# Eight gate products moved from the gate steps into four projections, and branch B's results read before the merge

## The chip, the core and the metric

The kernel runs on one core of one Trainium2 chip. The metric is the device time of one execution in microseconds (us), from the device's own clock. The kernel before took 1479.22 us (median of three runs, 1477.01 to 1479.26).

## What is computed

One layer of an encoder with 1024 tokens of width 1024, and 16 meta tokens ahead of them (1040 rows). All inputs are float32. The part that matters here is the mixer:

```python
proj = h @ w_in                     # qa, ka, va, qb, kb, vb, ga, gb
y_a = differential_attention(qa, ka, va, ...)   # 4 heads, all keys
y_b = windowed_gqa(qb, kb, vb, sink)            # 8 heads, 2 key heads, window 128
merged = jax.nn.sigmoid(ga) * (y_a @ w_ba) + jax.nn.sigmoid(gb) * (y_b @ w_bb)
h = h + merged @ w_o
h = h + (jax.nn.silu(n @ w_gate) * (n @ w_up)) @ w_down     # n = rms_norm(h)
out = rms_norm(h)
```

Here h is normalised ahead of the first product. The gates ga and gb are the columns of w_in from 2304 and from 3328 on, 1024 each.

## The kernel before

**Operands.** Every product runs in fp32r with split operands: a float32 tile is split into a rounded high part (on ACT, ScalarE) and the remainder as low part (on POOL, GpSimd, or on DVE, VectorE), in `split` (L118 to L120). A product is then three matmuls: high by high, high by low, low by high. The normalised, transposed input lies in SBUF as hT_hi and hT_lo.

**Projections.** `prep` (L176) reads 128 columns of w_in into a tile w and splits them into wh and wl; there are two of each. `ensure` prepares the next entry of the list `order`, one projection ahead of the one that runs; entries in `on_vector` are split on DVE, the others on POOL. `project_a(h)` projects q, v and k of head h of branch A. The results leave PSUM by ACT and DVE into tiles of `stage` (tag qk, three rooms, named qk_stage, va_stage and gate_first) and go to DRAM by DMA (qa_d, va_d, ka_d). All DMAs are issued by SP, in an order fixed when the program is built; each DMA takes one of eight completion semaphores in turn and waits for the DMA eight before it.

**Gate products.** ga and gb are not computed in a plain way but with seven products instead of eight for each 2 x 2 block of blocks. The two gates are cut into 8 groups k of 256 columns; for each there are products p = 1 to 7, each of 128 columns by 512 tokens over 512 rows. Some take sums of weight blocks (ws_d, prepared on POOL during branch B, `weight_sums`) and sums of token blocks (ts_d, `token_sums`, read over a quarter of hT by `load_sums` when that quarter is no longer needed). Product p = 2 takes no sums: weights of rows 512 to 1023, first 128 columns of the group, and tokens as they are (`quad(., 1, 0)`). One product is four steps of three matmuls with 512 columns; `gate_steps` (L716) is a generator of such steps, `g_load` reads the weights of a product (tile gr, five rooms), `g_split` splits them into gop (four rooms), and the result goes to g_d in DRAM, by an ACT copy, or by an addition on DVE to what g_d held (gk).

**What runs when.** Branch B's attention overlaps the projections of heads 2 and 3 of branch A (POOL's order is the written one there, other engines are ordered by a scheduler when the program is built). Then come the products of p = 2 with k = 0 to 3 (w_g, w_gop, L699 and L744: `G_EARLY`), then those with k = 4 to 7 (gr, gop, `G_FIRST` = 16 steps) ahead of head 0's first score, then attention of branch A: 32 tiles of 128 queries, in which PE's order is written by hand. `SLOTS` says in which order a tile's score chunks (s), gate steps (g), transposes (t) of the tile before, and value products or the tail (n) follow each other; `SLOTS_MORE` has one gate step more and is used for the first four tiles. Heads 1 to 3 begin with `G_HEAD` = 10 gate steps. `HOLD` = 30 steps are kept for the tail, after the last tile (L911). In the iteration after tile 31 (only transposes) no step is left.

**Merge.** After the gate steps y_b @ w_bb and y_a @ w_ba are computed (`branch_mm`, L769, PSUM tile ppa), each multiplied with its sigmoid. Branch B's results have been in DRAM (yb_d) since before attention. They are read into four rows of the tile tb (L958) and split into yb (L964), and the first two weight blocks of w_bb are read into another part of tb (L954). tb lies in room that attention used. The other weight blocks and y_a are read into a ring that lies where hT was, so these DMAs wait for the last gate matmul.

Of the kernel before, what the change touches and what calls it, by code (L numbers as in the profile page):

```python
# [19 lines left out]
P = 128  # L20
# [20 lines left out]
SLOTS_MORE = "sgsgsngsgsgstntnt"  # L41
# [6 lines left out]
HOLD = 30  # L48
N_MORE = 4
# [3 lines left out]
G_FIRST = 16  # L53
G_EARLY = 4
# [21 lines left out]
def encoder_block(ctx: ExitStack, tc: tile.TileContext, x, meta, norm_mix, w_in, lq1, lk1, lq2, lk2,  # L76
# [117 lines left out]
    on_vector = order[on_vector:] + [C_QB]  # L194
    prepped = {}

    def ensure(n):
        while order and len(prepped) < n:
            col = order.pop(0)
            prepped[col] = prep(col, f"c{col}", lo_eng=nc.vector if col in on_vector else None)  # L200
# [59 lines left out]

    vtpool, close_vt = pool("vtpool")
    lowpool, close_low = pool("lowpool")
    bpool, close_bpool = pool("bpool")
    kb = [(bpool if g else lowpool).tile([P, 2, NT, 144], F32R, tag=("k1", "kb")[g], name=f"kb{g}", bufs=1) for g in range(BG)]
    vb = [(bpool if g else lowpool).tile([P, 9, P], F32R, tag=("q1", "vb")[g], name=f"vb{g}", bufs=1) for g in range(BG)]
# [313 lines left out]
    G_ACT = {2: (1, 0), 5: (0, 1), 3: (1, 1), 1: (0, 0), 6: (1, 0), 7: (0, 1), 4: (1, 1)}  # L579
    G_OUT = {2: (0, 0), 5: (1, 1), 3: (0, 1), 1: (0, 0), 6: (0, 1), 7: (1, 1), 4: (1, 0)}  # L580
    order_g = [(2, k) for k in range(8)]
# [35 lines left out]
    def g_load(n, raw=None):  # L617
        p, k = order_g[n]
        if raw is None:
# [3 lines left out]
                          g_weights(k, *{2: (1, 0), 1: (0, 0), 4: (1, P)}[p], P))  # L623
# [33 lines left out]
    def load_a1(h):  # L657
        q = [None, lowpool.tile([P, S], F32R, tag="q1", name=f"aq{h}_1", bufs=1)]
# [52 lines left out]
    flush_v()  # L711
    order_pool.__exit__(None, None, None)

    gpools = []

    def gate_steps():  # L716
        for n, (p, k) in enumerate(order_g):
            if gpools:
                g_ahead(n + 1)
            op, act = g_ready.pop((p, k)), G_ACT[p]  # L720
            if p in (2, 5, 1):
                g_bank[k] = pp_bank(f"pg{p}_{k}")
            ps = g_bank[k]
            for c in range(4):
                for i, (a, b) in enumerate(((0, 0), (0, 1), (1, 0))):
                    nc.tensor.matmul(ps, op[:, a, c], quad(b, *act)[:, c], start=(p in (2, 5, 1) and c == 0 and i == 0),  # L726
                                     stop=(p in (2, 3, 4) and c == 3 and i == 2), skip_group_check=True)
                if c == 3:
# [3 lines left out]
                    else:  # L732
                        if gpools:
                            st = gpool.tile([P, 512], F32, tag="g", name="gate_stage", bufs=G_BUFS)
                        else:
                            st = f32(stage.tile([P, 2, 512], F32R, tag="qk", name="gate_first", bufs=QK_BUFS))[:, 0]
# [8 lines left out]
    for _ in range(4 * G_EARLY):  # L745
        next(gates)
# [5 lines left out]
    gpools.append(gpool)  # L752
# [3 lines left out]
    apool2, close_apool2 = pool("apool2")  # L756


    def branch_w(p, o, src, nme, raw=None):
        w = (raw_tile(f"wbr{nme}_{o}")[:, 0:512] if raw is None else raw).rearrange("p (c n) -> p c n", n=P)  # L760
        nc.sync.dma_start(w, src[:, o * P:(o + 1) * P].rearrange("(c p) n -> p c n", p=P))
# [87 lines left out]

    n_gates = [4 * (len(order_g) - G_EARLY) - HOLD]  # L850

# [28 lines left out]
    for n in range(AH * NT + T_LAG):  # L880
        scoring, turning = iter(()), iter(())
        if n < AH * NT:
# [5 lines left out]
            if t % 2 == 0:  # L888
                at_ = apool2.tile([P, 9, 2, 256], F32R, tag="at", name=f"at{h}_{t}", bufs=AT_BUFS)
# [5 lines left out]
        for what in SLOTS_MORE if n < N_MORE else SLOTS:  # L895
# [8 lines left out]
        for _ in scoring:  # L904
            pass
        for _ in turning:
# [3 lines left out]
    n_gates[0] += HOLD  # L910
    while tail:  # L911
        step_tail()
        fill(3)
    order_pe.__exit__(None, None, None)
    close_apool2()
    close_apool()
    close_low()
    close_vt()
    fill(1000)
    ypool, close_ypool = pool("ypool")  # L920
    close_psum2()
# [28 lines left out]
    tb = ypool.tile([P, DC, S], F32, name="tb")  # L950
    ya0pool, close_ya0 = pool("ya0pool")
    ybpool, close_yb = pool("ybpool")

    first_w = [branch_w(ypool, o, w_bb, "b", tb[:, 2, o * 512:o * 512 + 512]) for o in range(2)]  # L954

    yb_t = []
    for j in range(4):
        nc.sync.dma_start(tb[:, 4 + j, :], yb_d[j])  # L958
        yb_t.append(ybpool.tile([P, 2, S], F32R, name=f"yb{j}"))
        if j % 2:  # L960
            for h in range(2):
                cols = slice(h * 512, h * 512 + 512)
                for k in (j - 1, j):
                    split(yb_t[k][:, 0, cols], yb_t[k][:, 1, cols], tb[:, 4 + k, cols], nc.vector)  # L964
# [31 lines left out]
    for o in range(DC):  # L996
        w = first_w[o] if o < 2 else branch_w(ypool, o, w_bb, "b")
        for half in range(2):
            gt, ps, tk = gated(0, o, half, w, yb)
            nc.vector.tensor_tensor(tb[:, o, tk], gt, ps, ALU.mult)  # L1000
# [15 lines left out]
    for n, (o, half) in enumerate(order_a):  # L1016
# [4 lines left out]
        nc.gpsimd.tensor_tensor(gt, gt, tb[:, o, tk], ALU.add)  # L1021
# [5 lines left out]
    close_ypool()  # L1027

# [461 lines left out]
```

## Time and profile before

| | |
|---|---|
| median of three runs | 1479.22 us |
| the profiled execution | 1477.96 us |
| its span, first to last instruction | 1476.2 us |
| PE busy | 1435.2 us, 97% |
| DVE, ACT, POOL busy | 60%, 46%, 44% |
| mean granted clock of TensorE | 0.988 |
| PE waits, by far the largest group (first gate products) | 8.4 + 6.7 us |

The stages by PE's timeline: branch B with the projections to 306, the products of p = 2 to 353, attention to 621, its tail with the last gate steps to 645, the merge from 649. How to read the views: a wait is listed as "engine, tile, line <- what it waited for: us in total, times, longest us". A line of a timeline has start, duration, engine, line, operation, output <- inputs, shape and count; in brackets stands the idle time before it and what ended it. A line of windows has the window, its length, the busy time and number of instructions of PE, PE's weight loads, DVE, ACT and POOL, then the granted clock, the share of the DMA engines and GB/s. L119 and L120 are the two lines of `split`, for whatever tile. Rows of a busy PE overlap, since matmuls are pipelined; the distance of starts is the pace.

### The profile page before, as it was taken

How to read it: one execution, taken by the hardware profiler on the slowest of the kernel's cores; microseconds unless marked ns; L12 is line 12 of the kernel's file. 1: busy time of each engine (PE TensorE's matmuls, PEld its weight loads, DVE VectorE, ACT ScalarE, POOL GpSimd, SP SyncE). 2: the span in 40 equal slices, each digit the busy share in tenths (PEclk: the TensorE clock that was granted, in tenths of full speed). 3: DMA queues.
4: the chain of work that ended last, by engine and by line, in shares of the span. 5: the costliest groups of instructions: out<-in, count | busy, mean ns of one | idle time of the engine just before them, and what ended most of it. 6: DMA issues, size and time to landing. Idle time of an engine off the chain costs nothing.

```text
span 1476.2 us, 21253 instructions
## 1 busy us (share of the span) xinstructions
PE 1435.2 (97%) x7279; PEld 1226.9 (83%) x7279; DVE 888.0 (60%) x1618; ACT 682.0 (46%) x1293; POOL 650.7 (44%) x614
## 2 busy tenths in 40 slices
PE   8999999978999999999999999999999999999997
PEld 7998989966998899868788878888888888888886
DVE  7478436513879788743522876655555554777667
ACT  6366435524666555544511653333333333444454
POOL 5599127734333433333822475554544452000444
PEclk9999999989999999999999999999999999999999
DMA  8368768776276655277541433333322233964433
GB/s 240 87 204 240 211 167 252 236 245 232 94 247 205 225 176 173 74 251 219 182 149 58 142 110 127 128 107 101 107 100 98 96 107 107 325 217 135 130 124 140
DMA packets 189692, 242.42 MB, mean 164 GB/s; under 512 B 19008, under 2 KB 116736, under 8 KB 189584
## 3 DMA queue, kind: packets, MB, share of 16 engines
q1 hardware_dynamic: 189584, 241.07, 50.7%
q8 instruction: 57, 0.93, 0.3%
q14 instruction: 51, 0.42, 0.1%
HBM read 157.45 MB, written 77.00 MB: 159 GB/s over the span
## 4 chain that ended last, share of the span: by engine, by line
PE 79%; POOL 6%; DVE 5%; issue 4%; DMA 4%; ACT 1%; SPq 1%; POOLq 0%; ACTq 0%; DVEq 0%
PE pg L1271 27%; PE pg L726 9%; PE pd L1365 8%; PE po L1048 6%; PE ppa L769 5%; PE aps L785 4%; PE apy L824 3%; PE pp_qb L211 3%; POOL oa L120 3%; PE pp_va L211 2%; PE pp_qa L211 2%; PE apt L811 2%; PE pp_ka L211 1%; PE bpt L351 1%; PE bps L326 1%
## 5 line engine op out<-in xcount | busy, mean ns | idle before, releaser
L120 POOL TENSOR_TENSOR wop<-wf,wop 128x512 fp32r<-128x512 f32 x128 | 173.3, 1358 | 165.2 <-ACT wop L119 150.7
L1271 PE MATMUL pg<-t,wop 128*128 128x512 f32 x1056 | 242.6, 389 | 0.0
L1271 PEld LDWEIGHTS pg<-t,wop 128*128 128x128 f32 x1056 | 198.2, 188 | 41.2
L1365 PE MATMUL pd<-ob,oa 128*128 128x512 f32 x924 | 210.2, 389 | 0.7 <-POOL oa L120 0.4
L1365 PEld LDWEIGHTS pd<-ob,oa 128*128 128x128 f32 x924 | 173.3, 188 | 37.5 <-POOL oa L120 0.9
L1271 PE MATMUL pg<-b,wop 128*128 128x512 f32 x792 | 185.6, 392 | 2.3 <-DVE c L1280 2.3
L1271 PEld LDWEIGHTS pg<-b,wop 128*128 128x128 f32 x792 | 149.4, 189 | 34.2 <-issue 2.4
L726 PE MATMUL pg<-hT_hi,gop 128*128 128x512 f32 x416 | 154.8, 398 | 6.9 <-ACT gop L119 6.7
L120 POOL TENSOR_TENSOR gop<-gr,gop 128x512 fp32r<-128x512 f32 x52 | 68.6, 1321 | 135.7 <-ACT gop L119 135.6
L120 POOL TENSOR_TENSOR oa<-ra,oa 128x512 fp32r<-128x512 f32 x33 | 44.1, 1336 | 170.6 <-ACT oa L119 169.2
L119 ACT ACTIVATE wop<-wf 128x512 fp32r<-128x512 f32 x128 | 80.2, 632 | 84.3 <-PE pg L1271 51.7
L119 ACT ACTIVATE oa<-ra 128x512 fp32r<-128x512 f32 x77 | 48.6, 632 | 106.7 <-PE pd L1365 48.9
L726 PEld LDWEIGHTS pg<-hT_hi,gop 128*128 128x128 f32 x416 | 79.1, 190 | 20.1 <-ACT gop L119 7.2
L793 ACT ACTIVATE as<-as,amn 128x1040 f32<-128x1040 f32 x64 | 74.6, 1165 | 44.0 <-DVE amn L788 37.0
L785 PE MATMUL aps<-ak,aq 128*128 128x392 f32 (+1 forms) x384 | 89.9, 327 | 0.3 <-DVE yg L846 0.3
L1048 PE MATMUL po<-woh,mT 128*128 128x512 f32 x384 | 88.0, 390 | 0.0
L1048 PEld LDWEIGHTS po<-woh,mT 128*128 128x128 f32 x384 | 71.9, 188 | 14.8
L1106 DVE TENSOR_TENSOR s<-wf,wf 128x512 f32<-128x512 f32 x22 | 18.7, 848 | 107.9 <-DMA wf<-in_w_ff_gate_dram 54.8
L726 PE MATMUL pg<-hT_lo,gop 128*128 128x512 f32 x208 | 82.8, 398 | 0.0
L785 PEld LDWEIGHTS aps<-ak,aq 128*128 128x128 f32 x384 | 69.6, 188 | 13.2 <-DVE at L815 0.5
L338 POOL TENSOR_SCALAR bs<-bs,bdn 128x432 f32<-128x432 f32 (+1 forms) x64 | 41.5, 668 | 84.0 <-DVE bdn L336 68.3
L788 DVE CUSTOM_DVE_ANT_0 as<-aps,dist,far_a 128x392 f32<-128x392 f32 x64 | 39.6, 618 | 54.7 <-PE aps L785 54.3
(278 smaller groups left out, 3086.7 us busy)
## 6 DMA issues: line engine op xcount, KB each, us to landing
ra<-aop SPq DMA_DIRECT2D x77, 256.0 KB, 2.6
wf<-in_w_ff_gate_dram SPq DMA_DIRECT2D x24, 512.0 KB, 3.7
wf<-in_w_ff_up_dram SPq DMA_DIRECT2D x24, 512.0 KB, 3.6
aop<-as SPq DMA_DIRECT2D x44, 256.0 KB, 2.1
w_c<-in_w_in_dram SPq DMA_DIRECT2D x17, 512.0 KB, 6.1
aop<-c SPq DMA_DIRECT2D x33, 256.0 KB, 2.0
ts_d<-to SPq DMA_DIRECT2D x16, 512.0 KB, 3.7
gw<-in_w_in_dram SPq DMA_DIRECT2D x32, 256.0 KB, 4.2
```

The source lines that it names most:

```text
L119: nc.scalar.activation(hi, src, AF.Copy)
L120: lo_eng.tensor_tensor(lo, src, f32(hi), ALU.subtract)
L211: nc.tensor.matmul(ps[:, :n], a[:, c, :], b[:, c, at:at + n], start=(c == 0 and i == 0), stop=(c == DC - 1 and i == 2))
L338: nc.gpsimd.tensor_scalar(st[:, r, :W], st[:, r, :W], dn[:, r:r + 1], 1.0, ALU.mult, ALU.mult)
L726: nc.tensor.matmul(ps, op[:, a, c], quad(b, *act)[:, c], start=(p in (2, 5, 1) and c == 0 and i == 0), stop=(p in (2, 3, 4) and c == 3 and ...
L769: nc.tensor.matmul(ps, w[:, a, j, :], src(j, b, tk), start=(j == 0 and n == 0), stop=(j == 3 and n == 2))
L785: nc.tensor.matmul(ps[:, :n], qs[m][:, t * P:(t + 1) * P], ks[m][:, vv, k0:k0 + n], start=(vv == 0), stop=(vv == 1))
L793: nc.scalar.activation(s[m][:, 0:L], s[m][:, 0:L], AF.Exp, bias=low, scale=-1.0, accum_out=dn[:, m:m + 1])
L824: nc.tensor.matmul(py[:, cols], v[:kp, a, k, :], at_[:kp, k, b, :], start=(k == 0 and j == 0), stop=(k == 8))
L1048: nc.tensor.matmul(ps, mT[:, c, a, t * P:(t + 1) * P], wos[q, c][:, b], start=(c == 0 and n == 0), stop=(c == DC - 1 and n == 2))
L1271: nc.tensor.matmul(ps, op[:, x, c, :], b[:, y, c, :], start=(p in (1, 2, 5) and c == 0 and n == 0), stop=(p in (4, 2, 3) and c == 3 and n ...
L1365: nc.tensor.matmul(ps[u], oa[:, a, u * P:(u + 1) * P], ob[:, b, :], start=(p in (1, 2, 5) and j == 0 and k == 0), stop=(p in (2, 3, 4) and ...
```

## The change

The eight products of p = 2 leave the list of gate steps. Their weights become four more entries of the projections' list, each a pair of groups (k, k+1): two DMAs of 256 KB fill one w tile, which is split as the weights of a projection are, on DVE for (0, 1) and (2, 3), on POOL for the others. Eight runs of twelve matmuls (L720) go through the projections' PSUM banks and the three stage rooms (gate_first). Ahead of attention only the weights of the first two products of p = 5 are loaded and split (w_g, w_gop). `G_FIRST` is 0 and `SLOTS_MORE` is gone. `HOLD` is 26, and the iteration after tile 31 gets four gate steps ahead (`G_LAST`) and four by its slots, so the tail has 26 steps.

The lowest pool keeps two rooms, k1 and k0 (the last head's keys), until after the merge. When tile 31 is scored, yb_d is read into these rooms as yb_raw; its splits come ahead of the end of the gate steps. The first two blocks of w_bb are read into rooms of gr during the tail. The rows of tb that yb_d took before are now the yb_raw tiles (`tb_row`).

```diff
-HOLD = 30
-N_MORE = 4
+HOLD = 26
-G_FIRST = 16
-G_EARLY = 4
+G_FIRST = 0
+G_LAST = 4
...
-        nc.sync.dma_start(w, w_in[:, col:col + P].rearrange("(c p) n -> p c n", p=P))
+        if isinstance(col, tuple):
+            for i, k in enumerate(col):
+                nc.sync.dma_start(w[:, 4 * i:4 * i + 4], g_weights(k, 1, 0, P))
+        else:
+            nc.sync.dma_start(w, w_in[:, col:col + P].rearrange("(c p) n -> p c n", p=P))
...
-    on_vector = order[on_vector:] + [C_QB]
+    on_vector = order[on_vector:] + [C_QB, (0, 1), (2, 3)]
+    order += [(k, k + 1) for k in range(0, 8, 2)]
...
-    order_g = [(2, k) for k in range(8)]
+    order_g = []
...
-    for n in range(G_EARLY):
-        g_load(n, tpool.tile([P, 512], F32, tag="ta", name=f"w_g{n}", bufs=3))
-        g_split(n, tpool.tile([P, 2, 4, P], F32R, tag="to", name=f"w_gop{n}", bufs=2))
-    g_done[:] = [G_EARLY, G_EARLY]
...
+    for k in range(0, 8, 2):
+        ensure(1)
+        wh, wl = prepped.pop((k, k + 1))
+        for i in range(2):
+            ps = pp_bank(f"pg2_{k + i}")
+            for c in range(4):
+                for j, (a, b) in enumerate(((wh, 0), (wh, 1), (wl, 0))):
+                    nc.tensor.matmul(ps, a[:, 4 * i + c], quad(b, 1, 0)[:, c], start=(c == 0 and j == 0), stop=(c == 3 and j == 2))
+            st = f32(stage.tile([P, 2, 512], F32R, tag="qk", name="gate_first", bufs=QK_BUFS))[:, 0]
+            nc.scalar.copy(st, ps)
+            nc.sync.dma_start(g_place(2, k + i), st)
+        ensure(W_BUFS - 1)
+    for n in range(2):
+        g_load(n, tpool.tile([P, 512], F32, tag="ta", name=f"w_g{n}", bufs=3))
+        g_split(n, tpool.tile([P, 2, 4, P], F32R, tag="to", name=f"w_gop{n}", bufs=2))
+    g_done[:] = [2, 2]
...
+            if n == AH * NT - 1:
+                yb_raw = [lowpool.tile([P, 2, S], F32, tag=f"k{m}", name=f"yb_raw{m}", bufs=1) for m in (1, 0)]
+        else:
+            fill(G_LAST)
...
+        if n == AH * NT - 1:
+            for j in range(4):
+                nc.sync.dma_start(yb_raw[j // 2][:, j % 2], yb_d[j])
...
+        if g_done[0] == len(order_g) and not raw_w:
+            raw_w += [gpool.tile([P, 512], F32, tag="gr", name=f"raw_w{o}", bufs=GR_BUFS) for o in range(2)]
+            for o in range(2):
+                load_w(raw_w[o], o, w_bb)
...
-        nc.sync.dma_start(tb[:, 4 + j, :], yb_d[j])
...
+    for h in range(2):
+        cols = slice(h * 512, h * 512 + 512)
+        for j in range(4):
+            split(yb_t[j][:, 0, cols], yb_t[j][:, 1, cols], yb_raw[j // 2][:, j % 2, cols], nc.vector)
```

**ACT between the last projection and attention.** The rows below are in the order of the built program; tile names end in a number that tells them apart, gate_first has none, pg_k is the PSUM bank of group k, wh_c_3833 belongs to groups 2 and 3, wh_c_3872 to 4 and 5, wh_c_3911 to 6 and 7. Before:

```order
L360 COPY by_1_7_3217<-bpy_7_3187 64x512
L229 ACTIVATE qk_stage<-pp_ka_0_3733 128x384
L119 ACTIVATE w_gop_3771<-w_g_3769 128x512
L119 ACTIVATE w_gop_3776<-w_g_3774 128x512
L737 COPY gate_first<-pg_0_3810 128x512
L119 ACTIVATE w_gop_3781<-w_g_3779 128x512
L119 ACTIVATE w_gop_3786<-w_g_3784 128x512
L737 COPY gate_first<-pg_1_3826 128x512
```

The same place now, on ACT:

```order
L117 ACTIVATE wh_c_3833<-w_c_3830 128x1024
L232 ACTIVATE qk_stage<-pp_ka_0_3735 128x384
L722 COPY gate_first<-pg_0_3798 128x512
L365 COPY by_1_7_3219<-bpy_7_3189 64x512
L117 ACTIVATE w_gop_3949<-w_g_3947 128x512
L117 ACTIVATE wh_c_3872<-w_c_3869 128x1024
L722 COPY gate_first<-pg_1_3814 128x512
L722 COPY gate_first<-pg_2_3837 128x512
L117 ACTIVATE w_gop_3954<-w_g_3952 128x512
L117 ACTIVATE wh_c_3911<-w_c_3908 128x1024
L722 COPY gate_first<-pg_3_3853 128x512
```

The splits of w_g (now of p = 5) have moved between the copies, each with the split of a projection's weights behind it. PE's order at product 4 is, with all numbers of the names:

```order
L720 MATMUL pg2_3_3853<-hT_hi_135,wl_c2_3834 128x512
L720 MATMUL pg2_4_3876<-hT_hi_135,wh_c4_3872 128x512
L720 MATMUL pg2_4_3876<-hT_lo_136,wh_c4_3872 128x512
L720 MATMUL pg2_5_3892<-hT_hi_135,wh_c4_3872 128x512
L720 MATMUL pg2_5_3892<-hT_lo_136,wh_c4_3872 128x512
L720 MATMUL pg2_6_3915<-hT_hi_135,wh_c6_3911 128x512
L720 MATMUL pg2_6_3915<-hT_lo_136,wh_c6_3911 128x512
L720 MATMUL pg2_4_3876<-hT_hi_135,wl_c4_3873 128x512
```

Two matmuls each of products 4, 5 and 6 stand ahead of the first with a low part of the weights.

**SP at the start of attention.** The rows are DMA issues; ws_d_95 to 98 are the weight sums of groups 0 to 3, ts_d_92 the token sums of p = 6, which wait for the last matmul of p = 2. Now:

```order
L723 DMA g_d_87<-gate_first 128x512
L582 DMA hT_lo<-ts_d_92 128x4x512
L582 DMA hT_hi<-ts_d_92 128x4x512
L723 DMA g_d_89<-gate_first 128x512
L627 DMA gr_0_3965<-ws_d_95 128x512
L627 DMA gr_1_3967<-ws_d_96 128x512
```

Before, the weights of four products of p = 2 and the first ones of p = 5 stood at the corresponding place:

```order
L738 DMA g_d_81<-gate_first 128x512
L622 DMA gr_4_3889<-in_w_in_dram 128x4x128
L622 DMA gr_5_3891<-in_w_in_dram 128x4x128
L622 DMA gr_6_3893<-in_w_in_dram 128x4x128
L622 DMA gr_7_3895<-in_w_in_dram 128x4x128
L622 DMA gr_0_3897<-ws_d_95 128x512
```

The token sums of p = 6 have moved ahead of the first loads for p = 3.

**ACT at the end of the gate steps.** Before, the splits of yb stood behind the last copy of a gate product (pg_7):

```order
L119 ACTIVATE gop_7_7202<-gr_7_7175 128x512
L737 COPY gate_stage<-pg_6_7003 128x512
L119 ACTIVATE wbhb_7300<-tb 128x512
L119 ACTIVATE wbhb_7304<-tb 128x512
L737 COPY gate_stage<-pg_7_7119 128x512
L119 ACTIVATE yb_7308<-tb 128x512 x2
```

Now they stand ahead of the last gate operand (of these eight splits the last three are shown):

```order
L117 ACTIVATE yb_7309<-yb_raw_6940 128x512
L117 ACTIVATE yb_7310<-yb_raw_6941 128x512
L117 ACTIVATE yb_7311<-yb_raw_6941 128x512
L117 ACTIVATE gop_7_7197<-gr_7_7170 128x512
L748 COPY gate_stage<-pg_6_7053 128x512
L117 ACTIVATE wbhb_7282<-raw_w_7184 128x512
L117 ACTIVATE wbhb_7285<-raw_w_7185 128x512
L748 COPY gate_stage<-pg_7_7084 128x512
```

The splits of yb have moved from behind the last copy to ahead of the split of the last gate operand; those of the first merge weights (wbhb) stay ahead of the last copy.

More of the change, by code (lines that the diff above doesn't have):

```diff
@@ L725, in gate_steps @@
                 for i, (a, b) in enumerate(((0, 0), (0, 1), (1, 0))):
-                    nc.tensor.matmul(ps, op[:, a, c], quad(b, *act)[:, c], start=(p in (2, 5, 1) and c == 0 and i == 0),
-                                     stop=(p in (2, 3, 4) and c == 3 and i == 2), skip_group_check=True)
+                    nc.tensor.matmul(ps, op[:, a, c], quad(b, *act)[:, c], start=(p in (5, 1) and c == 0 and i == 0),
+                                     stop=(p in (3, 4) and c == 3 and i == 2), skip_group_check=True)
                 if c == 3:
@@ L732, in gate_steps @@
                     else:
[L733 to L736, printed above, removed]
+                        st = gpool.tile([P, 512], F32, tag="g", name="gate_stage", bufs=G_BUFS)
                         nc.scalar.copy(st, ps)
@@ L920, in encoder_block, with tb_row @@
     ypool, close_ypool = pool("ypool")
+    tb = [ypool.tile([P, 4, S], F32, name="tb"), *yb_raw]
+    first_w = [branch_w(ypool, o, w_bb, "b", raw_w[o]) for o in range(2)]
+    def tb_row(o, tk):
+        return tb[0][:, o, tk] if o < 4 else tb[o // 2 - 1][:, o % 2, tk]
     close_psum2()
```

58 lines of the change are left out of this document (26 added, 32 removed).

## The prediction

> **What bounds the kernel now.** I read the page first: TensorE (PE) is busy in nearly all of the span, so only PE's idle time and its slow clock can be won.
>
> ```profile
> PE 1435.2 (97%) x7279; PEld 1226.9 (83%) x7279; DVE 888.0 (60%) x1618; ACT 682.0 (46%) x1293; POOL 650.7 (44%) x614
> ```
>
> The span is 1476.2 us, so PE idles for 41 us. Next I read the waits of PE (what it waited for: us in total, times, longest).
>
> ```profile
> PE pg L726 <- ACT w_gop L119: 8.4, 2, 5.5
> PE pg L726 <- ACT gop L119: 6.7, 1, 6.7
> PE apt L811 <- DVE as L799: 3.5, 3, 2.1
> PE ppa L769 <- ACT yb L119: 3.3, 1, 3.3
> ```
>
> Three of the four are at places that the change rewrites: the first gate products wait for their split weights (8.4 + 6.7 us), and the merge waits for branch B's split results (3.3). Of the third, one wait of 2.1 us is at the last transposes of attention, where no gate step is left. Together they are 15.1 + 2.1 + 3.3 = 20.5 us. The timeline of PE gives the places.
>
> ```profile
> 306.03 1.53 PE L357 MATMUL bpy<-btr,vb 128*128 128x512 f32 x5
> ...
> 353.03 0.52 PE L785 MATMUL aps<-ak,aq 128*128 128x392 f32 x2
> ...
> 363.76 1.14 PE L811 MATMUL apt<-ident,as 128*128 128x128 f32 x9
> 364.77 0.62 PE L785 MATMUL aps<-ak,aq 128*128 128x392 f32 x2
> ...
> 644.92 0.39 PE L726 MATMUL pg<-hT_lo,gop 128*128 128x512 f32 x1
> 645.15 0.40 PE L726 MATMUL pg<-hT_hi,gop 128*128 128x512 f32 x1
> 648.80 0.79 PE L769 MATMUL ppa<-yb,wbhb 128*128 128x512 f32 x1 [3.25 <-ACT yb L119]
> ```
>
> From 306.03 (the end of the last projection) to 353.03 (the first score) PE runs the 8 gate products of p=2, 96 matmuls. A matmul of 512 columns takes 0.23 us (644.92 to 645.15), so this is 22.1 us of work, with the 1.5 us of bpy ahead 23.6, done in 47.0. The rest is waiting and slow clock. I read the clock in windows behind each wait; the column after POOL is the granted clock.
>
> ```profile
> 313.00:317.00 4.00, 3.85 (x9) 2.63 (x10) 0.00 (x0) 0.63 (x1) 1.46 (x2) 0.55 0.53 143
> 323.70:330.00 6.30, 6.14 (x14) 4.37 (x15) 0.00 (x0) 1.36 (x3) 5.65 (x14) 0.50 0.73 268
> 339.50:344.00 4.50, 4.35 (x10) 2.99 (x11) 0.00 (x0) 1.89 (x3) 4.28 (x4) 0.51 0.90 308
> 616.70:621.20 4.50, 4.47 (x25) 4.50 (x26) 1.38 (x3) 1.36 (x3) 0.00 (x0) 0.62 0.00 0
> ...
> 648.80:652.00 3.20, 3.20 (x6) 1.58 (x6) 2.57 (x4) 2.27 (x5) 0.00 (x0) 0.50 1.02 413
> 652.00:656.00 4.00, 4.00 (x14) 2.81 (x13) 2.82 (x5) 3.88 (x6) 0.00 (x0) 0.68 1.05 404
> ```
>
> One minus the clock, times the window, is lost: 1.8 + 3.2 + 2.2 before attention, 1.7 at its end, 1.6 + 1.3 = 2.9 in the merge. So each of the waits costs again about half of itself or more. What the change can win at most is 15.1 + 7.2 = 22.3 before attention, 2.1 + 1.7 = 3.8 at its end and 3.3 + 2.9 = 6.2 in the merge: 32 us. TensorE's work itself stays the same (as many matmuls of each size), so everything turns on how much of these 32 us is really given back, and what is late next.
>
> **Step 1, the gate products before attention.** They no longer wait for a chain of w_g load, split on ACT and split on POOL; the weights come through the projections' buffers, and those of the first four products are split before or while the last projection runs. What is late next is the way out: each product is copied by ACT into one of three stage tiles, whose earlier contents must have been written out, and ACT works in order. I walk it with these rows (timeline of ACT, of DVE, of SP's queue; DMA issues from 296 to 320 with KB and median us to landing; ACT's splits of 1024 columns, mean 1056 ns):
>
> ```profile
> 311.56 0.49 ACT L229 ACTIVATE qk_stage<-pp_ka 128x384 fp32r<-128x384 f32 x1 [3.39 <-DMA va_d<-va_stage]
> 312.33 0.63 ACT L119 ACTIVATE w_gop<-w_g 128x512 fp32r<-128x512 f32 x1 [0.28 <-DMA w_g<-in_w_in_dram]
> ```
>
> ```profile
> 312.09 0.56 DVE L230 TENSOR_TENSOR qk_stage<-pp_ka,qk_stage 128x384 fp32r<-128x384 f32 x1 [3.19 <-ACT qk_stage L229]
> ```
>
> ```profile
> 305.44 2.54 SPq L548 DMA_DIRECT2D ka_d<-qk_stage  x2
> ...
> 312.96 0.58 SPq L622 DMA_DIRECT2D w_g<-in_w_in_dram  x1
> ```
>
> ```profile
> w_g<-in_w_in_dram SPq DMA_DIRECT2D x4, 256.0 KB, 4.8
> ...
> ka_d<-qk_stage SPq DMA_DIRECT2D x4, 192.0 KB, 5.8
> ```
>
> ```profile
> L119 ACT ACTIVATE wh_c<-w_c 128x1024 fp32r<-128x1024 f32 x11 | 11.6, 1056 | 17.8 <-PE pp_qb L211 9.3 <-PE pp_va L211 3.7 <-PE pp_qa L211 3.3
> ```
>
> Products 0 and 1 with the bpy matmuls run from 306.0 to 306.0 + 1.5 + 24 x 0.23 = 313.0 without a wait. Product 2 needs the bank that DVE leaves at 312.09 + 0.56 = 312.7: it runs to 315.8. Product 3 needs the bank of product 0. ACT is held until 311.56, as now, by the write-out of va_stage; then the copy of product 0 needs the stage tile of ka_d, issued until 308.0 and 5.8 on its way: 313.8, copied by 314.4. So product 3 runs to 318.5. Now ACT's order matters: ahead of product 1's copy stand the split of the first w_g of p=5 and the split for products 4 and 5. That w_g is issued at about 313 and takes 4.8: 318, its split 0.6, the other split 1.06, the copy 0.6: PE can start product 4 at 320 to 321, after 2 us of waiting. Of products 4, 5 and 6 PE's order has only two matmuls each before it turns back to product 4, and those of product 6 need the split for 6 and 7 and the copy of product 3, both behind the split of the second w_g, whose load is issued after product 0's write-out on SP and lands at about 323.5: 323.5 + 0.6 + 1.06 + 0.6 = 325.8. So PE idles about 1.5 to 2.4 and then 4 us. What is left then is 44 matmuls, 10.1 us, with about 2 us of slow clock (a window above costs 1.8 to 3.2): the first score at **338** instead of 353.0, a gain of **15.0**. Bounds: 330 without any wait (306.0 + 23.6), 345 if the w_g loads or the write-outs come 3.5 us later each; both ends are kept.
>
> [...]
>
> **Step 2, the start of attention.** No gate product stands ahead of the first head any more, and the second group of products (p=3) has no weights loaded. SP issues the 2 MB of token sums for p=6 first, then the last write-out, then the weights for p=3, k=0. In before, loads of such weights stood beside those 2 MB too:
>
> ```profile
> hT_hi<-ts_d SPq DMA_DIRECT2D x1, 1024.0 KB, 9.5
> gr<-ws_d SPq DMA_DIRECT2D x2, 256.0 KB, 7.4
> ```
>
> ```profile
> L120 POOL TENSOR_TENSOR gop<-gr,gop 128x512 fp32r<-128x512 f32 x52 | 68.6, 1321 | 135.7 <-ACT gop L119 135.6
> ```
>
> Issued about 2 us after the first score and 7.4 to 9.5 under way, they land at +9.4 to +11.5; with the split of 0.63 the first matmul can go at +10 to +12.1, and the third one, which needs POOL's 1.3, at +13.4 at the latest. They are needed as follows: from 353.03 to 363.76 PE did two tiles of scores and 10 gate steps; 10 x 0.69 = 6.9, so the scores are 3.8. Now it is 8 steps: 5.5 + 3.8 + the transposes (1.0) + one score pair (0.4) = +10.7. The wait is 0 to 2.7; I take 2 and a slow clock of 1. DVE has little room in these tiles to catch up:
>
> ```profile
> 372.00:378.00 6.00, 6.00 (x37) 5.35 (x36) 5.93 (x18) 3.97 (x9) 2.32 (x3) 1.00 0.33 122
> ```
>
> With fewer gate steps per tile PE waits for DVE's 5.9 of 6 us here and there, 0 to 1. Step 2 costs **+3.5** (0 to +5).
>
> [...]
>
> **Step 3, the end of attention.** Eight gate steps (5.5 us) now lie in the last iteration, where PE waited 2.1 us for the last scores and lost 1.7 of clock. They cover both: **-3.8** (0 at worst). The tail has 26 steps instead of 30, 17.9 us. Eight yb splits of 0.64 on ACT stand in it ahead of the last gate operand, 5.1 + 0.64 + 1.3 = 7.1 us, which 17.9 us hide; that cover gone, it would cost up to 1. I put **+0.5**.
>
> **Step 4, the merge.** The chain of waits now runs through the read of branch B's results and their first split:
>
> ```profile
> 642.18 5.86 DMA tb<-yb_d
> ...
> 648.12 0.64 ACT yb L119
> ```
>
> ```profile
> wbrb<-in_w_branch_b_dram SPq DMA_DIRECT2D x6, 256.0 KB, 5.9
> ```
>
> The reads and splits move ahead of the last gate step; only the copy of the last product is between it and the first merge matmul, on another bank. So the 3.3 and 2.9 go: -6.2. What is late next are the weights of the third output block. Their loads still wait for the last gate matmul (they lie over hT) and stand behind four raw_ya reads; with 2.5 us of issuing and 5.9 under way they land at +8.4 to +9.5, split by +10.4 to +11.5, needed after 48 matmuls at +11.0. So 0 to 0.5, and I put **-5.7** (0 to -6.2). Behind it the order of work is as before.
>
> **The sum.** -15.0 + 3.5 - 3.8 + 0.5 - 5.7 = -20.5. The profiled execution took 1477.96 us, its span 1476.2; 1478.0 - 20.5 = 1457.5. The median of the runs, 1479.22, lies 1.3 above the profiled one, so I say **1458**.
>
> **Rivals.** (a) The four projections run without waits, first score at 330: 8 more, 1450. For it: the banks and stage tiles are free but for one load each. Against: ACT's order puts two loads ahead of copies that PE needs. (b) The chain through ACT and the stage tiles is longer, first score at 345: 1465. For it: the DMA engines can be full (a share of 1.02 in the window from 648.8), and every write-out goes through them. (c) The merge keeps its loss, as the weights of the third block are as late as yb was: 1464. For it: 0.5 us of margin only. (d) The change doesn't do what it says: the extra projections wait for their own loads as w_g did, first score still near 350: 1470. Against: these loads are issued two projections ahead. (e) **Slower**: attention starves from its start. The place is SP's queue at the first score: if each gate operand's load takes 8.9 us (between the 7.4 and 9.5 above) against tiles of 5.7 (half of 5.5 + 3.8, and 1.0), each product waits 3.2 and loses 1.7 of clock, 4.9 per product; it decides from five products in a row on (24 us of gain without step 2's own cost), and with eight the time is 1478 - 24 + 39 = 1493. Against: five raw buffers are filled at once, and after the 2 MB nothing large follows, so that one product should wait, not eight.
>
> **How the numbers follow.** Forecast 0.50; (a) 0.12; (b) 0.18; (c) 0.10; (d) 0.05; (e) 0.05. From 1449 to 1470 holds the first four, 0.90, less some spill at the ends. A measurement of this kernel can tell 0.2% (3 us) from no change. Faster 0.92: all but (e) and part of (d); within 0.2% 0.03; slower 0.05.
>
> **What would show it.** Right: in PE's waits w_gop and the 6.7 us of gop are gone, and a few us on ACT's copies (gate_first) or wh_c stand at products 4 to 6; first score at 335 to 341; one wait on gop or gr 10 to 13 us later; the clock 1.00 at 616 and in the merge's first window; ppa begins within 0.5 us of the last pg. Wrong: first score beyond 345, a wait on wbhb or raw_ya of over 2 us in the merge, or repeated waits on gop in the first ten tiles.

## The result and the profile after

The changed kernel takes 1455.3 us (median of four runs, 1454.01 to 1456.41), the kernel before 1478.19 us in the same series (1477.01 to 1479.26): a ratio of 0.9845, 95% interval 0.9828 to 0.9862, 22.9 us less. 1458 was predicted, 1449 to 1470 as range. The profiled execution of the changed kernel took 1455.1 us, its span is 1453.3 us, with a mean granted clock of 0.995 instead of 0.988.

The waits of PE, after (longest groups first):

```profile
PE pg L720 <- ACT gate_first L722: 3.5, 3, 2.7
...
PE ppa L783 <- POOL wbha L118: 1.3, 1, 1.3
...
PE pg L740 <- POOL gop L118: 0.8, 1, 0.8
PE apt L825 <- DVE as L813: 0.7, 1, 0.7
```

The groups w_gop (8.4 us) and yb (3.3) are gone, gop has fallen from 6.7 to 0.8, and in their place stand 3.5 us on the copies of the eight products, as forecast. The timeline of PE at the places of the prediction:

```profile
306.18 0.39 PE L720 MATMUL pg<-hT_hi,wh_c 128*128 128x512 f32 x1
...
320.13 0.50 PE L720 MATMUL pg<-hT_hi,wh_c 128*128 128x512 f32 x1 [0.62 <-ACT gate_first L722]
...
323.59 0.80 PE L720 MATMUL pg<-hT_hi,wh_c 128*128 128x512 f32 x1 [2.72 <-ACT gate_first L722]
...
336.51 0.53 PE L799 MATMUL aps<-ak,aq 128*128 128x392 f32 x2
...
349.13 0.51 PE L740 MATMUL pg<-hT_hi,gop 128*128 128x512 f32 x1 [0.85 <-POOL gop L118]
...
627.75 0.40 PE L740 MATMUL pg<-hT_hi,gop 128*128 128x512 f32 x1
627.98 8.35 PE L783 MATMUL ppa<-yb,wbhb 128*128 128x512 f32 x36
```

The windows (after the length the busy us of PE, its weight loads, DVE, ACT and POOL, then the granted clock) show, up to the merge, a single stretch of slow clock, around the end of the wait of 2.72 us, and none at the end of attention or in the merge:

```profile
318.00:323.60 5.60, 2.11 (x8) 0.80 (x6) 0.00 (x0) 3.34 (x6) 2.82 (x2) 0.90 0.98 303
323.60:329.30 5.70, 5.70 (x13) 4.45 (x14) 0.00 (x0) 0.14 (x1) 4.39 (x3) 0.50 0.77 274
...
600.00:604.70 4.70, 4.70 (x31) 4.16 (x31) 1.62 (x2) 1.23 (x2) 2.19 (x2) 1.00 0.94 312
...
628.00:632.00 4.00, 4.00 (x19) 3.31 (x18) 0.69 (x1) 3.13 (x4) 1.13 (x1) 1.00 0.97 304
```

The rows of the score tiles and of the merge's second half give the other marks: the last score starts at 610.8 before and 594.2 after, the first matmul of y_a @ w_ba at 695.6 and 671.5. (Count, then shortest, median and longest in ns, then first and last start; the first two lines are of the kernel before.)

```profile
L785 PE MATMUL aps<-ak,aq x384: 275/339/450, 353.0 to 610.8; 128*128 128x392 f32 x128, 128*128 128x256 f32 x64
L769 PE MATMUL ppa<-ya,wbha x192: 387/389/496, 695.6 to 740.3; 128*128 128x512 f32 x192
...
L799 PE MATMUL aps<-ak,aq x384: 275/340/448, 336.5 to 594.2; 128*128 128x392 f32 x128, 128*128 128x256 f32 x64
...
L783 PE MATMUL ppa<-ya,wbha x192: 387/389/504, 671.5 to 716.5; 128*128 128x512 f32 x192
```

So the 22.9 us come from here (marks in us of the span; four gate steps, 2.8 us of work, have moved from the row "first to last score" to the one below it):

| stretch | before | after | difference | of it waits and clock | forecast |
|---|---|---|---|---|---|
| start to first score | 353.0 | 336.5 | -16.5 | -16.5 | -15.0 |
| first to last score | 257.8 | 257.7 | -0.1 | +2.7 | +3.5 |
| last score to last gate matmul | 34.4 | 33.5 | -0.9 | -3.6 | -3.3 |
| from there to y_a @ w_ba | 50.5 | 43.8 | -6.7 | -6.7 | -5.7 |
| the rest | 780.6 | 781.8 | +1.2 | +1.2 | 0 |

The rest contains two slightly longer waits (1.3 instead of 1.0 on wbha, 1.2 instead of 0.3 on ob). The change touches neither, and both differ as much between the profiles below: 0.4 to 2.1 on wbha, 0.4 to 1.4 on ob.

ACT's timeline in the first stretch is the chain that the prediction walked:

```profile
313.37 0.59 ACT L722 COPY gate_first<-pg 128x512 f32<-128x512 f32 x1 [2.14 <-DMA ka_d<-qk_stage]
313.98 0.58 ACT L365 COPY by<-bpy 64x512 f32<-64x512 f32 x1
316.54 0.63 ACT L117 ACTIVATE w_gop<-w_g 128x512 fp32r<-128x512 f32 x1 [1.97 <-DMA w_g<-ws_d]
317.08 1.04 ACT L117 ACTIVATE wh_c<-w_c 128x1024 fp32r<-128x1024 f32 x1
318.14 0.59 ACT L722 COPY gate_first<-pg 128x512 f32<-128x512 f32 x1
319.49 0.59 ACT L722 COPY gate_first<-pg 128x512 f32<-128x512 f32 x1 [0.76 <-DMA ka_d<-qk_stage]
321.49 0.63 ACT L117 ACTIVATE w_gop<-w_g 128x512 fp32r<-128x512 f32 x1 [1.41 <-DMA w_g<-ws_d]
322.02 1.04 ACT L117 ACTIVATE wh_c<-w_c 128x1024 fp32r<-128x1024 f32 x1
322.97 0.57 ACT L722 COPY gate_first<-pg 128x512 f32<-128x512 f32 x1
```

Each of the first four copies (lines 1, 5, 6 and 9) releases a PSUM bank, and two loads of w_g (1.97 and 1.41 us of idle ACT) and the write-outs of ka_d stand ahead of them. The last copy ends where PE's wait of 2.72 us ends.

### The profile page after: what moved, and what is told of

The parts are those of the page before. It is cut to its first block, busy times and chain, and to the rows that moved or that the text cites. A ratio compares the mean times of both kernels' runs of the same rounds, so it can differ in the third digit from the quotient of the medians.

```text
span 1453.3 us, 21234 instructions
## 1 busy us (share of the span) xinstructions
PE 1426.3 (98%) x7279; PEld 1221.7 (84%) x7279; DVE 899.0 (62%) x1620; ACT 680.3 (47%) x1289; POOL 647.3 (45%) x608
## 4 chain that ended last, share of the span: by engine, by line
PE 77%; POOL 6%; DVE 5%; issue 5%; DMA 4%; ACT 2%; SPq 1%; POOLq 0%; DVEq 0%; ACTq 0%
PE pg L1296 28%; PE pd L1390 8%; PE pg L740 7%; PE po L1073 6%; PE ppa L783 4%; PE aps L799 3%; PE apy L838 3%; PE pp_qb L214 3%; POOL oa L118 3%; PE pp_va L214 2%; PE pp_ka L214 2%; PE pp_qa L214 2%; PE apt L825 2%; PE bpt L356 1%; PE bpy L362 1%
## 5 line engine op out<-in xcount | busy, mean ns | idle before, releaser
L740 PE MATMUL pg<-hT_hi,gop 128*128 128x512 f32 x368 | 136.8, 395 | 0.8 <-POOL gop L118 0.8
L118 POOL TENSOR_TENSOR gop<-gr,gop 128x512 fp32r<-128x512 f32 x46 | 62.0, 1349 | 113.7 <-ACT gop L117 113.7
L1131 DVE TENSOR_TENSOR s<-wf,wf 128x512 f32<-128x512 f32 x22 | 27.7, 1261 | 105.3 <-DMA wf<-in_w_ff_gate_dram 56.8
L740 PEld LDWEIGHTS pg<-hT_hi,gop 128*128 128x128 f32 x368 | 69.2, 188 | 11.9 <-POOL gop L118 1.3
L740 PE MATMUL pg<-hT_lo,gop 128*128 128x512 f32 x184 | 72.6, 395 | 0.0
L810 POOL TENSOR_SCALAR as<-as,adn,neglam 128x1040 f32<-128x1040 f32 x32 | 39.0, 1218 | 60.6 <-DVE adn L808 34.0
```

Source lines behind the costliest of these rows:

```text
L118: lo_eng.tensor_tensor(lo, src, f32(hi), ALU.subtract)
```

## The experiments

All ratios are to the kernel before, measured in the same series; in the second and third series a yardstick was run beside the others. First the parts of the change, one by one.

| kernel | median us | ratio (95% interval) |
|---|---|---|
| changed kernel | 1455.3 | 0.9845 (0.9828 to 0.9862) |
| yb read late | 1462.1 | 0.9896 (0.9878 to 0.9914) |
| no steps in the last iteration | 1456.0 | 0.9861 (0.9844 to 0.9879) |
| gate products as before | 1469.83 | 0.9950 (0.9936 to 0.9964) |
| no read of the sums of p=6 | 1454.64 | 0.9847 (0.9828 to 0.9866) |
| changed kernel again | 1454.54 | 0.9843 (0.9818 to 0.9869) |
| low parts on DVE | 1450.05 | 0.9818 (0.9792 to 0.9843) |
| high parts of w_g on DVE | 1452.62 | 0.9833 (0.9807 to 0.9859) |
| both on DVE | 1451.16 | 0.9824 (0.9798 to 0.9850) |
| PE's order only | 1450.74 | 0.9820 (0.9806 to 0.9835) |
| low parts on DVE, five steps early | 1452.96 | 0.9833 (0.9819 to 0.9846) |
| low parts on DVE again | 1449.69 | 0.9807 (0.9792 to 0.9822) |

**Branch B's results read late.**

```diff
-    tb = [ypool.tile([P, 4, S], F32, name="tb"), *yb_raw]
+    tb = ypool.tile([P, DC, S], F32, name="tb")
...
+    for j in range(4):
+        nc.sync.dma_start(tb[:, 4 + j, :], yb_d[j])
```

> The changed kernel with branch B's results read into tb after attention again, as before; the first two blocks of w_bb still come early, the gate products stay projections. Theory (each place gives its own gain): the merge's 3.4 us of wait and 3.3 of slow clock come back, so 1455.3 + 6.7 = 1462, and ppa waits again on ACT's yb split, with the clock near 0.5 behind it. Rival 1 (reading w_bb early was the larger part, since the two reads stood ahead of yb on SP): only 1 to 3 us come back, 1457 to 1458. Rival 2 (the gain came from the gate products alone): no change, 1455.

Measured: 0.9896 against 0.9845, which is 7.5 us. The wait of the merge is back:

```profile
PE ppa L783 <- ACT yb L117: 3.7, 1, 3.7
...
L783 PE MATMUL ppa<-yb,wbhb x192: 387/389/796, 635.8 to 682.4; 128*128 128x512 f32 x192
```

From its last gate matmul (631.6) to y_a @ w_ba (682.6) it takes 51.0 us, against 43.8 in the changed kernel: 7.2, of which 3.9 is the longer gap up to 635.8 and 3.3 slower matmuls behind it (the longest takes 796 ns, the median one 389; the longest before, at a clock of 0.50, took 796 ns too). The theory holds, both rivals fall: w_bb came early here too, and it helped nothing alone. (This profiled execution, 1466.57 us against 1460.6 to 1462.1 in the three others, also lost 5 us between its first and last score. Its trace has 4.1 of them in two tiles early in head 2, 466 to 488 us: there DVE waits 4.3 us for a gate product read back into gk, 1.7 in the changed kernel, PE waits 0.78 and 1.12 us for DVE, and the clock is 0.86 on the mean from 470 to 482.5. Why that read came late is not shown.)

**No gate step in the iteration after tile 31.**

```diff
-HOLD = 26
+HOLD = 34
-G_LAST = 4
+G_LAST = 0
```

> The changed kernel with no gate step in the iteration after tile 31 (G_LAST 0, HOLD 34): the eight steps go to the tail. Theory: the wait of 2.1 us for the last scores returns, with a clock of 0.6 behind it, so +3.8: 1459. Rival (the tail's own waits, for gate operands and gk, get shorter with eight steps more, or PE finds the scores done by then): 0 to 1, 1455 to 1456.

The wait is back, but the slow clock is not (timeline and windows of this kernel):

```profile
599.78 0.63 PE L825 MATMUL apt<-ident,as 128*128 128x128 f32 x4 [1.81 <-DVE as L813]
```

```profile
600.00:604.00 4.00, 4.00 (x30) 3.71 (x29) 1.57 (x3) 1.36 (x3) 0.00 (x0) 1.00 0.61 220
```

From the last score to the last gate matmul (594.1 to 629.6) it is 35.5 us against 33.5: 2.0. The runs give 0.9861 against 0.9845, with intervals that overlap; so neither 3.8 nor 0 to 1, but half, and the timing alone can't settle it. The profiled execution is also the fastest of the four (1454.64 to 1459.47), so the others may have had a slow clock at this place that it did not. Before, a wait of 2.13 us at this place was followed by a clock of 0.62; a wait shorter by 0.3 was not.

**The gate products as before.** Products of p=2 are gate steps again, as before the change (G_EARLY 4, G_FIRST 16); the merge and the last iteration stay changed.

```diff
-    order += [(k, k + 1) for k in range(0, 8, 2)]
-    order_g = []
+    order_g = [(2, k) for k in range(8)]
...
-G_FIRST = 0
+G_FIRST = 16
+G_EARLY = 4
```

> The changed kernel with the eight products of p=2 as gate steps again (four ahead of attention, 16 steps at its start), but with the early read of branch B's results and the eight steps in the last iteration. Theory: only the gains at the end of attention (3.7) and in the merge (6.7) are left, 1478.2 - 10.4 = 1468, and PE waits 8 us on w_gop and 6.7 on gop again. Rival (the parts overlap; the early reads and splits only pay since the tail is shorter): 1472 or more.

Measured: 0.9950, 7.4 us below before, not 10.2. The waits at the start are back as expected,

```profile
PE pg L731 <- ACT w_gop L118: 8.5, 2, 6.3
PE pg L731 <- ACT gop L118: 6.7, 1, 6.7
```

and the first score is at 353.3. What is missing lies between the scores: 353.3 to 610.8 is 257.5 us, as long as before, although four steps (2.8 us) have left this stretch here too. So 2.5 us are lost here without any projection and without late weights of p=3, but not where the changed kernel loses its 2.7. The fourth tile of 128 queries starts (first scores of the first and the fourth tile here, then of the fourth tile in the changed kernel and before):

```profile
353.34 0.52 PE L796 MATMUL aps<-ak,aq 128*128 128x392 f32 x2
370.13 0.62 PE L796 MATMUL aps<-ak,aq 128*128 128x392 f32 x2 [0.18 <-DVE amn L799]
...
354.99 0.63 PE L799 MATMUL aps<-ak,aq 128*128 128x392 f32 x2 [0.22 <-DVE amn L802]
...
371.22 0.62 PE L785 MATMUL aps<-ak,aq 128*128 128x392 f32 x2
```

That is 16.8 us after the first score here, 18.5 in the changed kernel, and 18.2 before, with three gate steps (2.1 us) more ahead. So up to here 0.7 us are lost in this kernel and 2.4 in the changed one. By this comparison the steps taken out of the first tiles cost 0.7, and what the changed kernel loses beyond that comes with the wait on gop and behind it, so with its late weights. (That is argued from these rows; the next run, which should have taken the late weights away, does not settle it.) The rest of the 2.5 lies later, most of it in one wait of 1.34 us for DVE early in head 2 (491.79), a wait that is 0.68 us long at the same place in the changed kernel (475.05). The early read's part is whole: from the last gate matmul (644.3) to y_a @ w_ba (688.5) 44.2 us against 50.5, 6.3 less.

**No read of the sums of p=6.** The 2 MB at the start of attention are left out, so the products of p=6 use unsummed tokens.

```diff
-                        load_sums(later_p, *G_ACT[later_p])
+                        if later_p != 6:
+                            load_sums(later_p, *G_ACT[later_p])
```

> The changed kernel without the read of the token sums of p=6 (2 MB at the start of attention); the products of p=6 are computed on the unsummed tokens, so this part of the gates is another. Theory: these 2 MB hold back the weights of p=3; without them the wait on gop 12 us after the first score (0.85 us) and about as much behind it go: 1 to 2 us less, 1453.3 to 1454.3. Rival (the start of attention is held by DVE's work per tile, or by the stage room that the weights' room lies on): no change, 1455.3.

The time is the same (0.9847), but this run tells less than it should: without these DMAs the scheduler put other orders on POOL and ACT (POOL splits four gop, 340.58 to 345.91, ahead of its second work on as, which stands ahead of them in the changed kernel). The wait on gop is gone, and a longer one, on DVE's end of the first tile, stands 12 us after the first score (334.69), with the clock at 0.53 around its end:

```profile
347.07 2.18 PE L826 MATMUL apt<-ident,as 128*128 128x128 f32 x9 [2.85 <-DVE as L814]
```

```profile
347.00:350.00 3.00, 2.93 (x13) 2.88 (x14) 1.94 (x9) 1.52 (x3) 1.21 (x1) 0.53 0.71 248
```

In its profile the slow clock in the first stretch also ended earlier at a like wait (2.76 and 2.72 us): matmuls are 0.43 us apart until 325.80, 2.7 us after the wait, against 5.7 us in the changed kernel. So its total says little about attention. What the 2 MB cost by themselves stays open.

Then the first stretch, where PE still loses 3.5 us of waiting and 2.9 of clock. As a yardstick the changed kernel again:

> The changed kernel once more, as the yardstick for the other kernels of this series: 0.9845 of before again, first score at 336 within 1 us.

It gave 0.9843, first score at 336.64. Since the stretch ahead differs between executions (the first matmul of the gate products comes at 305.3 to 307.9 us in the kernels of this part), the kernels of this part are best compared from the first matmul of the gate products to the first score: 30.3 us in the changed kernel's profile (306.2 to 336.5), 29.6 in this one (307.0 to 336.6). The work alone, 96 matmuls of 0.23 and 1.5 of bpy, is 23.6 us.

**Low parts of groups 4 to 7 on DVE.** The edit has a second effect: in the program that is built with it, PE finishes product 4 before it takes up 5 and 6. (In the kernel before, the low part of such a tile took 1.2 us on DVE and 2.4 on POOL; that the scheduler's choice comes from this is not shown.)

```diff
-    on_vector = order[on_vector:] + [C_QB, (0, 1), (2, 3)]
+    on_vector = order[on_vector:] + [C_QB, (0, 1), (2, 3), (4, 5), (6, 7)]
```

> The changed kernel with the low parts of the weights of groups 4 to 7 on DVE instead of POOL; the program then has PE finish product 4 before product 5 and 6, in place of two matmuls of each. Theory (PE stands since it needs the bank and weights of product 6 after only four matmuls, not since the chain through ACT is long as such): products 4 and 5, 5.5 us of work, cover the time to 323.6 until product 6 can go; about 1 us of waiting is left ahead of product 4, the clock stays at 1.00, first score at 331 to 332 instead of 336.5, 4.5 to 5.5 us less in all: 1450. Rival (the chain through ACT, the w_g loads and the stage rooms sets the pace of every product): the waits only move, first score at 335 to 337, 1454 to 1455.

1450.05 us, 4.5 less than the yardstick of this series. The first score is at 330.21, 23.4 us after the first gate matmul (306.8), with no wait of PE and a clock of 1.00 all along:

```profile
318.00:324.00 6.00, 6.00 (x28) 4.86 (x27) 2.71 (x2) 3.36 (x6) 1.45 (x2) 1.00 1.01 300
324.00:330.00 6.00, 6.00 (x28) 4.86 (x27) 0.00 (x1) 1.18 (x2) 0.00 (x0) 1.00 0.81 297
```

And ACT's chain is nearly as late as it was: its second wait for w_g ends at 320.91, 14.1 us after the first gate matmul, against 15.3 in the changed kernel.

```profile
320.91 0.63 ACT L117 ACTIVATE w_gop<-w_g 128x512 fp32r<-128x512 f32 x1 [2.08 <-DMA w_g<-ws_d]
```

**High parts of the two w_g on DVE.** PE's order stays, the loads no longer stand in ACT's way.

```diff
-        split(op[:, 0], op[:, 1], g_raw.pop((p, k)), nc.gpsimd)
+        split(op[:, 0], op[:, 1], g_raw.pop((p, k)), nc.gpsimd, n < 2)
```

(With the last argument true, `split` writes the high part on DVE.)

> The changed kernel with the high parts of the first two w_g of p=5 split on DVE, so that ACT has no wait for these two loads between the copies; PE's order keeps two matmuls each of products 4 to 6. Theory (ACT's order puts two loads ahead of copies): the copies of products 1 to 3 come 1.5 to 2 us earlier, held now only by the write-out of ka_d (319.4) for product 2; PE's wait falls from 3.5 to about 2 and the slow clock behind it is shorter or gone: 2 to 4 us less, first score at 332.5 to 334.5. Rival (the stage rooms, not the loads, hold the copies): first score at 336, no change.

The first score is at 331.45, 26.1 us after the first gate matmul (305.3); PE waits twice, 0.73 and 1.42 us, and the clock stays at 1.00:

```profile
318.97 0.50 PE L723 MATMUL pg<-hT_hi,wh_c 128*128 128x512 f32 x1 [0.73 <-ACT gate_first L725]
...
321.11 0.50 PE L723 MATMUL pg<-hT_hi,wh_c 128*128 128x512 f32 x1 [1.42 <-ACT gate_first L725]
```

So this helps too, from the other side: 3.5 to 4.2 us less in this stretch, where 2 to 4 were expected, most of it the slow clock, which goes altogether with some 1 us less of waiting. Of this the timed runs show 1.9 us; in the profile some comes back between the scores (259.1 instead of 257.7).

**Both.**

> Both edits of the two runs before together. If PE's order is the cause, this adds 1 us at most to the gain of the low parts on DVE alone: first score at 330 to 331, 1449. If the chain through ACT is the cause, it is the first one that shows a gain beyond 2 us.

First score at 329.92, 23.4 us after the first gate matmul, 1451.16 us in all: nothing over the low parts on DVE alone that the runs can tell. Either edit removes the wait, the other then finds none.

**PE's order alone.** To part the two effects of the low parts on DVE: POOL keeps them, and PE's order in the eight products is the written one.

```diff
+    order_pe = tc.manual_schedule(engines={mybir.EngineType.PE})
+    order_pe.__enter__()
     for k in range(0, 8, 2):
```

> The changed kernel with one thing other: PE runs the eight products one after the other, as they are written; the low parts of groups 4 to 7 stay on POOL and ACT's order stays. Theory (PE's order was the larger cause): PE waits 1 to 2 us once, for POOL's low part of groups 4 and 5 (ACT's split at 317.1 to 318.1, POOL 2.4 us, so 320.6), and runs through from there with 46 matmuls: first score at 331 to 332, total 4 to 5 us below the changed kernel, within 1 us of the kernel with the low parts on DVE. Rival (POOL's 2.4 us per split was the cause): first score at 334 to 337, at most 2 us gained.

One wait of 0.81 us is left, for POOL's low part, at 320.85, and the first score is at 331.62, 24.5 us after the first gate matmul:

```profile
320.85 0.50 PE L722 MATMUL pg<-hT_hi,wl_c 128*128 128x512 f32 x1 [0.81 <-POOL wl_c L118]
```

1450.74 us, within 1.1 us of the low parts on DVE in the same series. ACT's chain is where it was: the copy of product 3 starts at 322.89, at 322.97 in the changed kernel. So of the two effects PE's order is the one that counts; POOL's 2.4 us cost 1.1 at most, 24.5 against 23.4.

**Five steps in the first four tiles again,** on top of the low parts on DVE:

```diff
-HOLD = 26
+HOLD = 22
+SLOTS_MORE = "sgsgsngsgsgstntnt"
+N_MORE = 4
```

> The kernel with the low parts on DVE, with five gate steps instead of four in each of the first four tiles again (SLOTS_MORE, HOLD 22). Theory (the first tiles lose since DVE's work per tile is longer than PE's with four steps): PE's idle time between the first and the last score falls by 1 to 1.5 us, so 1 us less in all. Rival (the weights of p=3 are late): the wait on gop grows by the time of the steps pulled ahead, and the total is the same or 1 to 2 us more.

3.3 us more than the yardstick, with intervals that just overlap: what the rival said, but only in part for its reason. The weights of p=3 are needed earlier and come no earlier, and the wait on gop grows (0.8 to 1.4); but between the first and the last score the profile has 262.4 us, with 2.8 us more of work, against 260.1 in the yardstick's, which is no loss. The loss lies behind: the tail, now four steps shorter, no longer covers the splits of yb and w_bb, and from the last gate matmul to y_a @ w_ba it takes 46.8 us instead of 44.2 (waits of PE in this kernel):

```profile
PE pg L742 <- ACT gop L119: 1.4, 1, 1.4
...
PE ppa L785 <- ACT wbhb L119: 1.2, 1, 1.2
...
PE ppa L785 <- POOL wbhb L120: 0.9, 2, 0.6
```

The yardstick of this series, the low parts on DVE once more:

> The kernel with the low parts on DVE once more, as the yardstick on this chip: 4.5 us below the changed kernel, first score at 330.

It gave 1449.69 us (0.9807), first score at 330.85. This version beats both kernels: some 28 us below before, 4.5 below the changed kernel in the series that had both.

## Why the prediction was right, point by point

- **Bounds.** The three places named were the three that gave: 16.5, 3.6 and 6.7 us of waits and clock, against 22.3, 3.8 and 6.2 that could be won. The last bound was 0.5 too low: by the starts of the matmuls the pause before was 3.4 us and the slow clock behind it cost 3.3. That each wait costs again half of itself or more was not so in the rows it was read from: 1.8 us behind 5.45 and 2.2 behind 6.72 are a third. All four steps came out better than forecast, by 0.3 to 1.5 us; the rest, forecast at nothing, took 1.2 back, so the total is nearer than the terms.
- **Step 1, right, 1.5 us too small.** The walk along ACT held: the copy of product 3, said to be done at 325.8, was done at 323.5, since both w_g loads landed 1.5 to 2 us earlier than 318 and 323.5. PE waited 3.5 us in three pieces where the walk has 5.5 to 6.4 in two, and the slow clock cost 2.9 (5.7 us at 0.50) instead of 2. The step also named PE's two matmuls of each product ahead of the wait; the runs show that this order is what makes a late copy cost anything: in PE's written order, with ACT's chain as late, PE waits 0.8 us, and that for a low part, and loses no clock.
- **Step 2, right, with its terms shifted.** 2.7 was lost, 3.5 forecast. The wait on gop came where it was said to be, 12.6 us after the first score, since the weights landed about when they were said to: issued 1.5 us after the first score, 7.8 under way. But "The wait is 0 to 2.7; I take 2 and a slow clock of 1" was too much: the wait was 0.85 (the work behind it came 1.1 late), with the clock at 1.00. The tile behind the wait took another 0.6 longer than with the gate products as before, and 0.7 go with fewer steps per tile, within the 0 to 1 that the step gave to waits for DVE; by the fourth tile this makes 2.4. Giving the steps back to the first tiles, while the weights stayed late, won nothing.
- **Step 3, right, but less its own than I had it.** 3.6 instead of 3.3. The wait alone is worth 2.0; the other 1.7 was a slow clock that a wait of 2.13 us brought and one of 1.81 did not, each in one profile. And since four of the eight steps for it were taken from the first tiles, where 2.7 were lost, if only 0.7 of it for this reason, steps 2 and 3 together won 0.9.
- **Step 4, right.** 6.7 instead of 5.7: the weights of the third output block came in time (their splits on ACT start at 637.08, 9.3 us after the last gate matmul), so the +0.5 was not needed. Reading w_bb early did nothing by itself. That the tail hides the splits is a matter of four steps: with 22 held back, PE waits 2.1 us for wbhb.
- **The rivals.** None came; (a), no waits in the projections, is what the kernels with one more edit reached: 1450, as it said, and the first score at 330.

## What to carry to other kernels

Work that waits for operands of its own is worth moving to a place where buffers, banks and split operands already flow, but look at what then leaves: here the write-out rooms and ACT, which waited 1.97 and 1.41 us for loads between its copies, set the pace. An engine that takes up several pieces of work at once, a few instructions each, needs all their buffers at the earliest: PE waited 3.5 us so, and 0.8 us when it finished one piece before the next, with ACT's copies as late. Filler work moved to cover one wait uncovers another place, so count both: eight steps at the end of attention won 3.6 us; the four of them that came from its start left 0.7 there, and taking four from the tail to give them back uncovered 2.6 us in the merge.

## What the runs showed of the hardware that was not expected

Whether a wait costs clock did not follow from its length alone. One wait is the same in all 13 profiles: in the FFN PE waits 2.0 us for the tile c and then runs 24 matmuls, 5.5 us of work at 0.23 each. In the kernel before and in the changed kernel they take 7.33 and 7.32 us. The low parts on DVE were profiled twice, and the two executions of this one kernel differ:

```profile
834.87 5.69 PE L1296 MATMUL pg<-b,wop 128*128 128x512 f32 x24 [2.02 <-DVE c L1305]
...
840.33 7.33 PE L1296 MATMUL pg<-b,wop 128*128 128x512 f32 x24 [2.02 <-DVE c L1305]
```

Of the 792 matmuls of this kind the longest takes 628 to 632 ns in nine of the 13 profiles, and 497 to 501 ns in the other four (no steps in the last iteration, no sums of p=6, low parts on DVE, both on DVE). The clock around this wait, in the changed kernel (wait from 838.92 to 840.92) and in the first execution of the low parts on DVE (832.85 to 834.87):

```profile
837.89:841.30 3.41, 1.41 (x7) 0.90 (x6) 3.41 (x6) 1.49 (x3) 2.19 (x1) 1.00 0.46 162
841.30:844.71 3.41, 3.41 (x10) 2.64 (x9) 3.41 (x6) 0.66 (x2) 0.01 (x1) 0.50 0.03 5
```

```profile
829.75:833.16 3.41, 3.10 (x14) 2.25 (x12) 3.41 (x7) 1.96 (x4) 0.11 (x1) 1.00 0.97 292
833.16:836.57 3.41, 1.70 (x8) 1.45 (x9) 3.41 (x6) 1.11 (x2) 2.08 (x1) 1.00 0.08 23
836.57:839.98 3.41, 3.41 (x17) 2.83 (x16) 3.41 (x7) 1.10 (x2) 0.39 (x1) 1.00 0.20 77
```

In the one the clock is 0.50 from 0.4 us after the wait on, in the other it stays at 1.00. What decides between them is not shown.

The waits of 2 us or more in the profiles of the kernel before and of the changed kernel, from 30 us on, and the stretch at a clock of 0.50 that was measured at each:

| kernel | wait | its end | clock 0.50 from | for |
|---|---|---|---|---|
| before | 5.45 us | 313.01 | 309.78 | 6.83 us |
| before | 2.94 us | 323.72 | 323.43 | 6.83 us |
| before | 6.72 us | 339.52 | 337.09 | 6.83 us |
| before | 2.13 us | 616.73 | 616.98 | 3.41 us |
| before | 3.25 us | 648.80 | 647.70 | 6.83 us |
| before | 2.01 us | 864.71 | 866.15 | 3.41 us |
| changed | 2.72 us | 323.59 | 322.48 | 6.83 us |
| changed | 2.00 us | 840.92 | 841.30 | 3.41 us |

Up to the last 10 us these two profiles have no other slow clock; their next longest waits, 1.02 us before and 1.32 us in the changed kernel, left it at 1.00. Nor did the wait of 1.81 us without steps in the last iteration bring one, nor the two of 0.73 and 1.42 us with the high parts of w_g on DVE. But with branch B's results read late the clock was 0.86 on the mean from 470 to 482.5, around waits of 0.78 and 1.12 us. So a slow clock of 3.41 or 6.83 us (by the clock, half of that is lost where PE is busy all along: 1.7 or 3.4 us) came with each wait of 2 us or more in these two profiles, and the wait of 2.02 us in the first execution of the low parts on DVE had none.
